# A hybrid attention, convolution and ConvFFN encoder on one core: SyncE's transfers in program order, and a new slot plan for the up product

## The chip, the cores and the metric

The kernel runs on one core of one Trainium2 chip, as one launch. The metric is device time in microseconds (us), lower is better. The same kernel is run several times and the median is taken; one further execution is profiled.

## The reference

Two layers over a residual stream of 1024 tokens by 1024 channels, float32. Cut to the part that the change touches:

```python
for l in range(DEPTH):                       # 2
    h = _rmsnorm(x, g_mix[l])
    p = h @ w_in[l]                          # latents, rope key, a and gate
    ...                                      # 8 heads of latent attention -> y_attn
    u = silu(layernorm(dwconv31(a * sigmoid(gt))))
    x = x + concatenate([y_attn, u]) @ w_o[l]
    h2 = _rmsnorm(x, g_ffn[l])
    z = _dwconv(h2 @ w_up[l], w_dw_ffn[l], b_dw_ffn[l])      # 1024 x 5632, 3 taps
    zg, zv = jnp.split(z, 2, axis=-1)                        # 2816 gates, 2816 values
    x = x + (silu(zg) * zv) @ w_down[l]
return _rmsnorm(x, g_final)
```

## The kernel before

**Stages.** Each layer runs projections, attention, the output product (`wo_steps`), the up product with the ConvFFN filter (`up_steps`) and the down product (`down_steps`). Channels lie on the partitions, tokens along the free dimension, in two halves of 512.

**The up product.** `w_up` is cut into 22 pairs of 128 columns: `f` from 0 to 21, with a gate tile (`e` = 0) and a value tile (`e` = 1) for each. Every pair is computed from seven products instead of eight (Strassen's scheme in Winograd's form over two halves of the contraction, gate and value columns): set `i` from 1 to 7 is a combination of halves of the activations (`self.sets[i]`, made once) times a combination of halves of the weights. One product is 12 matmuls of 512 columns: four blocks of the contraction, and for each high x high, high x low and low x high, because each operand is a pair of 16-bit numbers, a high half and a low half.

**Slots.** `feed` lays all products out as `steps`, one product per step (here called a slot). `put(step, rank, f)` hangs other work behind a slot, and within a slot the rank sorts it. `feed` emits slot by slot, so each engine's order is the order written by these numbers. The sequence of products is `seq`: first `START`, the pairs 0 to 3 ("opening pairs"), sets 1 and 2 of all four and then the other sets; then, for `f` from 4, a block of seven slots in the order of `ORDER = (1, 5, 6, 3, 7, 2, 4)`. With m the slot of set 1 of pair `f`, the table `UP` says where its preparation stands:

- `fetch` (m - 18): SyncE loads the raw gate tile (tag "wr", three buffers) and the raw value tile (tag "b", 31 buffers), 512 KB each; profile name `wu`, line L1106.
- `squares` (m - 15 and the next slot): ScalarE squares and sums each tile (`wsq`, L1128), for the scale of the 16-bit parts; `sum5` follows. TensorE's small product `own_total` (`wt`, L1161) and VectorE's `own_scale` (L1133) come at `total` and one slot later.
- for sets 5, 6, 3, 7, 4 two numbers: the slot of the high half (ScalarE, `part_hi`, `w`, L1182) and of the low half (VectorE, `part_lo`, L1185). Sets 1 and 2 are split together (`first_hi`, `first_lo`).
- `sum5`, `sum6`, `sum3`, `sum7`: GpSimd's accumulating loads that add another weight block into the raw tile (L1112), each between the low half of one set and the high half of the next.

The raw gate tile is last read by the low half of set 7; then its buffer is free for pair `f` + 3.

**After a product.** `evict` (the slot after) takes the bank: on ScalarE for sets 1, 5, 6 and 4 (L1228), on VectorE, adding, for 3, 7 and 2 (L1229). Sets 1, 6, 7 and 4 share one accumulating bank, 5 and 3 another, 2 has its own. Then the three-tap filter: its middle tap on ScalarE (L1618), two taps on VectorE (L1624), first for the gate, then, after a silu (L1260), for the value; `close` multiplies both (L1102) and SyncE stores the result (`act<-v`, L1268). For the opening pairs the filters are put off to the slots of `TAPS_AT`. Beside this, sums of the `w_down` weights for the down product are made on VectorE (`sum_load`, `sum_step`: `sd`, L1273 and L1102; stored as `ws`, L1281).

**The down product** is built alike from eleven slots per set. SyncE fetches its weights into the same three "wr" buffers (`fetch`, L1380) and loads the stored activations back (`load`, `ac<-act`, L1362).

**Who sets the order.** Four engines are in `MANUAL`: their instructions stand in the order in which the program emits them. SyncE is not among them; the order of its transfers is chosen by the scheduler. Each engine works in its order and waits at an instruction until what it needs is there.

Of the kernel before, what the change touches and what calls it, by code (L numbers as in the profile page):

```python
# [31 lines left out]
NF = DFF // 128  # L32
# [44 lines left out]
ROW_AT = {2: (7,)}  # L77
ROW_LATE = {0: (6,)}
E = mybir.EngineType
MANUAL = [E.PE, E.DVE, E.Activation, E.Pool]  # L80
LATE_KINDS = (("pool", "both", "act", "pool", "act"), ("pool", "both", "pool", "pool", "pool"))
LATE_COST = {"act": 1.1, "pool": 3.5, "both": 4.8}
NEAR_TAPS = (12, 14, 16, 14)
# [3 lines left out]
NPAR = P_BF + 2 * NF  # L87
HALVES = (slice(0, 512), slice(512, T))
ORDER = (1, 5, 6, 3, 7, 2, 4)
LEFT = 4  # L90
START = [(i, f) for f in range(LEFT) for i in (1, 2)]
START += [(i, f) for i in (5, 3, 6, 7, 4) for f in range(LEFT)]
MIX_AT = {5: (((19, 1), (20, 0.5)), ((20, 0.4), (21, 0.5))), 3: (((23, 0.6), (24, 0.6)), ((24, 0.5), (25, 0.6))),
          6: (((26, 0.6), (27, 0.6)), ((27, 0.5), (28, 0.6))), 7: (((30, 0.6), (31, 0.6)), ((31, 0.5), (32, 0.6))),
# [3 lines left out]
KEPT = 18  # L98
TAIL_STEPS = 6
FIRST_TOTAL = 7  # L100
TOTAL_AT = 32
TAPS_AT = (36, 39, 42, 46), (44, 48, 52, 57)
UP = {'fetch': -18, 'squares': -15, 'total': -13, 1: (-2, -2), 5: (-10, -9), 6: (-5, -4), 3: (0, 1), 7: (2, 3), 4: (-1, 0)}
SUM_AT = (0, 1, 2, 6)
LEFT_AT = {5: (15, 16, 18, 19), 6: (19, 21, 22, 23), 3: (24, 25, 26, 27), 7: (25, 31, 33, 34), 4: (37, 38, 39, 40)}
ENDS = (slice(512, 768), slice(768, T))
LEAD_HEADS = 3
# [26 lines left out]
class Encoder:  # L134
# [257 lines left out]
    def run(self):  # L392
# [11 lines left out]
        carry = None  # L404
        with self.tc.manual_schedule(engines=set(MANUAL)):
            for l in range(DEPTH):
# [687 lines left out]
    def up_steps(self, l, steps, put):  # L1094
        nc, a = self.nc, self.a
        left, right = HALVES
        seq = START + [(i, f) for f in range(LEFT, NF) for i in ORDER if (i, f) not in START]
        base = len(steps)
        at = {p: base + q for q, p in enumerate(seq)}
        self.kept = {}  # L1100
        raw, wts, zs, st, sums, scale, back, nback = defaultdict(dict), {}, defaultdict(dict), {}, {}, {}, {}, {}
# [28 lines left out]
        def scales(ps, out, w):  # L1130
            ps = ps.rearrange("p (f e) -> p f e", e=2)
            scale, back, nback, v, h = (out[:, i * w:(i + 1) * w] for i in range(5))
            nc.vector.tensor_reduce(out=v, in_=ps, op=ALU.add, axis=AX.X)  # L1133
            self.half_exponent(h, v)
            self.power(scale, h, -1.0, 204.0)
            for o, at in ((back, self.back), (nback, self.nback)):
                nc.vector.tensor_scalar(out=o.bitcast(I32), in0=h.bitcast(I32), scalar1=EXPONENT, scalar2=at, op0=ALU.mult, op1=ALU.add)
            return scale, back, nback

        def first_total():  # L1140
            ps = self.bank(f"wt{l}", (128, 2 * LEFT))
            tags = self.banks[1][0]
            tags.insert(0, tags.pop())
            nc.tensor.matmul(ps, self.ones, st["sums"], start=True, stop=True)
            parts = scales(ps, self.cp.tile([128, 5 * LEFT], F32, name=f"wt{l}", tag="wt", bufs=1), LEFT)
            for f in range(LEFT):
                scale[f], back[f], nback[f] = (t[:, f:f + 1] for t in parts)
# [97 lines left out]
        def filter_start(f, e):  # L1245
            z = zs[f]
            z["ov"[e]] = o = self.blk(f"{'ov'[e]}{l}_{f}")
            z["in", e] = z.pop("gv"[e]) if e == 0 else z["src"]
            self.conv_start(l, e * NF + f, o, z["in", e], 0, T)

        def filter_tap(f, e, t):
            z = zs[f]
            self.conv_tap(l, e * NF + f, z["ov"[e]], z["in", e], 0, T, t)

        def keep(f):
            zs[f]["src"] = zs[f].pop("v")

        def silu(f):
            o = zs[f]["o"]
            nc.scalar.activation(out=o, in_=o, func=AF.Silu)  # L1260

        def close(f):
            z = zs.pop(f)
            sub(z["v"], z["v"], z["o"], ALU.mult)
            if f >= KEPT:
                self.kept[f] = z["v"]
                return
            nc.sync.dma_start(out=self.actd[l][f], in_=z["v"])  # L1268

        def sum_load(j):  # L1270
            sums[j] = [self.blk(f"sd{l}_{j}{e}") for e in range(2)]
            for e, t in enumerate(sums[j]):
                nc.sync.dma_start(out=t, in_=a["w_down"][l, j + e * (NF // 2)])  # L1273

        def sum_step(j, n):
            p, q = sums[j]
            o, x = ((p[:, left], p[:, right]), (p[:, right], q[:, right]), (q[:, right], p[:, left]), (q[:, left], q[:, right]))[n]
            sub(o, o, x, ALU.add)
            if n == 3:
                for e, t in enumerate(sums.pop(j)):  # L1280
                    nc.sync.dma_start(out=self.wsd[l][j, e], in_=t)  # L1281

        def at_step(m, rank, g, *args):
            put(m, rank, lambda: g(*args))
# [11 lines left out]
        for f in range(LEFT):  # L1296
            at_step((13, 13, 15, 15)[f], 6 + f, sum5, f)
            for i, ms in LEFT_AT.items():
                m, g = ms[f], f % 2
# [4 lines left out]
        for q, (i, f) in enumerate(seq):  # L1304
            n = base + q
            steps.append(lambda i=i, f=f: product(i, f))
            m = EVICT.get((i, f), n + 1)
            put(int(m), m % 1 * 10, lambda i=i, f=f: evict(i, f))
        for f in range(LEFT, NF):
            n = m = at[1, f]  # L1310
            for e in range(2):
                at_step(m + UP["fetch"], 5 + e / 10, fetch, f, e, "b" if e else "wr")
                at_step(m + UP["squares"] + e, 2, own_squares, f, e)
            at_step(m + UP["squares"] + 1, 2.1, sum5, f)
            at_step(max(m + UP["total"], TOTAL_AT), 0.4, own_total, f)
            at_step(max(m + UP["total"], TOTAL_AT) + 1, 0.5, own_scale, f)
            for i in (5, 6, 3, 7, 4):
                hi, lo = (max(m + o, TOTAL_AT + 1) for o in UP[i])
                at_step(hi, 3.6, part_hi, i, f)
# [7 lines left out]
        for f in range(NF):  # L1327
            n = max(at[2, f], at[3, f], at[6, f]) + 1
            n = n if f >= LEFT else TAPS_AT[0][f]
            put(n, 3, lambda f=f: filter_start(f, 0))  # L1330
            put(n + 1, 3, lambda f=f: filter_tap(f, 0, 0))
            put(n + 2, 3, lambda f=f: filter_tap(f, 0, 2))
            put(n + 3, 4, lambda f=f: silu(f))
            m = max(at[7, f], at[4, f]) + 2 if f >= LEFT else TAPS_AT[1][f]
            put(m, 2.9, lambda f=f: keep(f))
            put(m, 3, lambda f=f: filter_start(f, 1))
            put(m + 1, 3, lambda f=f: filter_tap(f, 1, 0))
            put(m + 2, 3, lambda f=f: filter_tap(f, 1, 2))
            put(max(m + 3, n + 5), 3, lambda f=f: close(f))
        for j in range(NF // 2):  # L1340
            n = at[1, 7 + j * 13 // 11]
            put(n - 4, 5, lambda j=j: sum_load(j))
            for i, d in enumerate(SUM_AT):
                put(n + d, 4, lambda j=j, i=i: sum_step(j, i))

    def down_steps(self, l, steps, put):
        nc, a = self.nc, self.a
# [63 lines left out]
        def product(i, j, ms=range(4), cs=done):  # L1411
            b, t = pairs[i, j], BANK_SET[i]
            for m in ms:
                if i in (1, 5, 2) and j == 0:
                    ps[t, m] = self.pp.tile([128, 512], F32, name=f"pd{l}_{i}{m}", tag=f"d{4 * t + (m + 2) % 4}", bufs=1)
                for s, (p, q) in enumerate(((0, 0), (0, 1), (1, 0))):
                    nc.tensor.matmul(ps[t, m][:, cs], w[i, j][p][:, m * 128:(m + 1) * 128], b[:, q, cs],  # L1417
                                     start=(i in (1, 5, 2) and j == 0 and s == 0), stop=(j == half - 1 and s == 2),
                                     skip_group_check=i in (6, 7, 4, 3))
# [19 lines left out]

        order = [(i, j) for i in ORDER for j in range(half)]  # L1440
        at = {p: base + q for q, p in enumerate(order)}
# [27 lines left out]
        for c in range(2 if last else 0):  # L1469
            for m in range(4):  # L1470
                steps.append(lambda c=c, m=m: [product(4, j, (m,), cols[c]) for j in range(tail, half)])
        for i in ORDER[:-1]:
            for m in range(4):
# [581 lines left out]
```

## Time and profile before

| | us |
|---|---|
| median of 3 runs | 2264.53 |
| lowest and highest of them | 2263.61, 2265.57 |
| the profiled execution: its own time | 2264.85 |
| its span (first to last instruction) | 2263.0 |
| granted TensorE clock, mean | 0.999 of full speed |

Busy shares of the span: TensorE 99%, its weight loads 67%, VectorE 80%, ScalarE 60%, GpSimd 29%. In the profile a line such as L1221 is a line of the kernel; `out<-in` are tile names without buffer numbers; what stands behind "<-" in an idle time is the engine and the tile that ended it. In rows in order of time the columns are the start, the duration, the engine, the line, the operation, its tiles and shapes, the count of merged instructions, and in brackets the idle time ahead of it. SPq rows are SyncE's issues, and a merged row spans the first to the last of them with the waits between.

### The profile page before, as it was taken

How to read it: one execution, taken by the hardware profiler on the slowest of the kernel's cores; microseconds unless marked ns; L12 is line 12 of the kernel's file. 1: busy time of each engine (PE TensorE's matmuls, PEld its weight loads, DVE VectorE, ACT ScalarE, POOL GpSimd, SP SyncE). 2: the span in 40 equal slices, each digit the busy share in tenths (PEclk: the TensorE clock that was granted, in tenths of full speed). 3: DMA queues.
4: the chain of work that ended last, by engine and by line, in shares of the span. 5: the costliest groups of instructions: out<-in, count | busy, mean ns of one | idle time of the engine just before them, and what ended most of it. 6: DMA issues, size and time to landing. Idle time of an engine off the chain costs nothing.

```text
span 2263.0 us, 30127 instructions
## 1 busy us (share of the span) xinstructions
PE 2233.7 (99%) x10762; PEld 1511.4 (67%) x10762; DVE 1809.0 (80%) x2484; ACT 1349.5 (60%) x2076; POOL 659.2 (29%) x632
## 2 busy tenths in 40 slices
PE   9999999999999999999999999999999999999998
PEld 8887777784444444788888877777744444448887
DVE  7989888878888887776559798887798887878665
ACT  5355987646766665544533568786467666655444
POOL 1222788511111111001412237864111111110032
PEclk9999999999999999999999999999999999999999
DMA  6887998955589796835968989878646888868356
GB/s 192 171 182 251 196 205 176 267 152 117 134 231 257 202 255 163 295 102 138 210 142 167 212 252 208 182 158 246 168 108 158 236 244 223 241 162 284 103 123 171
DMA packets 176967, 434.81 MB, mean 192 GB/s; under 512 B 24769, under 2 KB 32817, under 8 KB 176817
## 3 DMA queue, kind: packets, MB, share of 16 engines
q0 software_dynamic: 79520, 176.31, 41.7%
q1 hardware_dynamic: 97008, 256.04, 33.5%
q8 instruction: 85, 1.39, 0.3%
q14 instruction: 66, 0.53, 0.1%
q10 hardware_dynamic: 288, 0.53, 0.1%
HBM read 293.56 MB, written 80.40 MB: 165 GB/s over the span
## 4 chain that ended last, share of the span: by engine, by line
PE 71%; DVE 12%; DMA 8%; ACT 4%; issue 4%; POOL 1%; SPq 0%; DVEq 0%; POOLq 0%; ACTq 0%
PE pd L1417 18%; PE p L1221 18%; PE s L1677 7%; DMA wu<-in_w_up 5%; PE po L956 5%; PE t L1717 4%; PE o L1740 4%; PE pa L234 2%; DVE w L1185 2%; DVE v L1624 2%; PE pg L234 2%; PE pg L552 2%; DVE conv L1892 2%; PE pq L234 1%; DVE sd L1102 1%
## 5 line engine op out<-in xcount | busy, mean ns | idle before, releaser
L1221 PE MATMUL p<-b,w 128*128 128x512 f16 x3696 | 807.6, 379 | 16.6 <-DVE w L1185 12.1
L1221 PEld LDWEIGHTS <-w 128*128 128x128 f16 x3696 | 360.3, 99 | 449.0 <-DVE w L1185 22.5
L1417 PE MATMUL pd<-ab,wd 128*128 128x512 f32 (+1 forms) x1920 | 422.7, 382 | 0.0
L1417 PEld LDWEIGHTS pd<-ab,wd 128*128 128x128 f32 x1920 | 350.7, 188 | 69.7 <-DVE ab L1612 0.4
L1112 POOL DMA_DIRECT2D wu<-in_w_up x176 | 153.7, 945 | 757.2 <-DVE w L1185 370.4
L1677 PE MATMUL s<-k,q 96*128 96x512 f32 x768 | 208.2, 406 | 3.3 <-DVE qn L748 3.0
L1128 ACT ACTIVATE wsq<-wu 128x1024 f16<-128x1024 f32 x88 | 92.3, 1050 | 179.8 <-DMA wu<-in_w_up 159.3
L1720 DVE SCALAR_TENSOR_TENSOR pt<-t,pt 128x512 f16<-128x512 f32 x256 | 164.7, 684 | 39.2 <-ACT pt L1719 38.6
L1185 DVE SCALAR_TENSOR_TENSOR w<-wu,wf,w 128x512 f16<-128x512 f32 (+1 forms) x216 | 177.4, 834 | 14.6 <-ACT w L1182 14.6
L1909 POOL TENSOR_TENSOR late<-gate,par 128x1014 f32<-128x1014 f32 (+12 forms) x79 | 172.4, 2182 | 12.8 <-PE pn L234 7.1
L1719 ACT ACTIVATE pt<-t 128x512 f16<-128x512 f32 x256 | 139.2, 595 | 56.8 <-PE t L1717 55.9
L1182 ACT ACTIVATE w<-wu,wf 128x512 f16<-128x512 f32 (+1 forms) x216 | 162.5, 783 | 6.9 <-DMA wu<-in_w_up 6.8
L1679 DVE TENSOR_REDUCE mx<-s 128x1 f32<-128x1024 f32 x128 | 155.6, 1215 | 1.3 <-PE s L1677 1.3
L1624 DVE SCALAR_TENSOR_TENSOR o<-zg,par,o 128x1023 f32<-128x1023 f32 x88 | 112.6, 1280 | 53.9 <-ACT o L1618 53.7
L1677 PEld LDWEIGHTS s<-k,q 96*128 96x128 f32 x768 | 135.8, 189 | 26.4 <-DVE qn L748 3.4
L1892 DVE SCALAR_TENSOR_TENSOR conv<-gate,par,conv 128x1009 f32<-128x1009 f32 (+7 forms) x112 | 142.2, 1274 | 3.7 <-ACT conv L614 1.0
L1687 ACT ACTIVATE p<-s,mx 128x1024 f32<-128x1024 f32 x128 | 143.3, 1119 | 2.6 <-DVE mx L1679 2.2
L1610 ACT CAST ab<-ac 128x512 fp32r<-128x512 f32 x130 | 80.0, 616 | 101.6 <-DVE ac L1351 64.3
L1717 PEld LDWEIGHTS t<-ident,p 128*128 128x128 f32 x1024 | 119.7, 141 | 25.1 <-DVE yt L1747 0.8
L1740 PE MATMUL o<-pt,v 128*128 128x512 f16 x512 | 132.8, 381 | 1.3 <-DVE pt L1720 1.1
L1717 PE MATMUL t<-ident,p 128*128 128x128 f32 x1024 | 133.2, 273 | 0.1
L918 POOL DMA_DIRECT2D wd<-in_w_down x44 | 31.8, 724 | 323.6 <-PE pd L1417 322.4
(2114 smaller groups left out, 3834.9 us busy)
## 6 DMA issues: line engine op xcount, KB each, us to landing
wu<-in_w_up SPq DMA_DIRECT2D x98, 512.0 KB, 5.9
wu<-in_w_up POOLq DMA_DIRECT2D x176, 256.0 KB, 4.7
sd<-in_w_down SPq DMA_DIRECT2D x44, 512.0 KB, 6.6
ws<-sd SPq DMA_DIRECT2D x44, 512.0 KB, 4.2
wd<-in_w_down POOLq DMA_DIRECT2D x88, 256.0 KB, 5.5
act<-v SPq DMA_DIRECT2D x36, 512.0 KB, 4.5
ac<-act SPq DMA_DIRECT2D x72, 256.0 KB, 5.8
wo<-in_w_o POOLq DMA_DIRECT2D x64, 256.0 KB, 7.5
```

Source lines behind the costliest of these rows:

```text
L1182: nc.scalar.activation(out=t, in_=src, func=AF.Copy, scale=scale[f])
L1185: nc.vector.scalar_tensor_tensor(out=t, in0=src, scalar=scale[f], in1=hi, op0=ALU.mult, op1=ALU.subtract)
L1221: nc.tensor.matmul(ps, w[p][:, k * 128:(k + 1) * 128], b[:, q], start=(i in (1, 5, 2) and k == 0 and t == 0), stop=(k == 3 and t == 2), sk ...
L1417: nc.tensor.matmul(ps[t, m][:, cs], w[i, j][p][:, m * 128:(m + 1) * 128], b[:, q, cs], start=(i in (1, 5, 2) and j == 0 and s == 0), stop= ...
L1624: self.nc.vector.scalar_tensor_tensor(out=o[:, a:b], in0=z[:, at + a:at + b], scalar=self.par[l][:, tap:tap + 1], in1=o[:, a:b], op0=ALU.m ...
L1677: nc.tensor.matmul(ps[:, cs], q[i][0:96, qs], k[j][0:96, cs], start=(s == 0), stop=(s == 2))
L1679: nc.vector.tensor_reduce(out=mx, in_=ps, op=ALU.max, axis=AX.X, negate=True)
L1717: nc.tensor.transpose(tp[:, i, qi * 128:(qi + 1) * 128], st["p"][2 * qp + qi][:, kt * 128:(kt + 1) * 128], self.ident)
L1720: nc.vector.scalar_tensor_tensor(out=lo, in0=tp, scalar=P_SCALE, in1=hi, op0=ALU.mult, op1=ALU.subtract)
L1740: nc.tensor.matmul(po, v[2 * c + i][:, h // 2, e, :], pt[s][:, 2 * (c % 2) + i, :], start=(c == 0 and i == 0 and s == 0), stop=(c == 3 and ...
L1892: self.nc.vector.scalar_tensor_tensor(out=y[:, lo:hi], in0=u[:, lo + s:hi + s], scalar=self.tap(l, j, t), in1=y[:, lo:hi], op0=ALU.mult, o ...
L1909: self.nc.gpsimd.tensor_tensor(out=p[:, lo:hi], in0=u[:, lo + s:hi + s], in1=self.tap(l, j, t).broadcast_to([128, hi - lo]), op=ALU.mult)
```

## The change

- SyncE is added to `MANUAL`, so its transfers stand in the order in which the program emits them, over the whole program. For that the two stores of `up_steps` get slots of their own: `act_store` and `sum_store`, one slot (`STORE_LAG`) after the work whose result they store.
- Blocks of the up product run in the order 1, 2, 6, 5, 7, 3, 4 (`UP_ORDER`); the down product keeps `ORDER`. The slots of the weights' halves are set anew in `UP`: sets 5, 6, 3 and 4 one slot later, set 7 one slot earlier. The squares and the total come one slot later; the loads stay at m - 18.
- `TAPS_AT`: gate filters of the opening pairs at 35, 37, 40, 46 instead of 36, 39, 42, 46, value filters at 41, 47, 54, 60 instead of 44, 48, 52, 57.
- `START` begins with set 1 of pairs 0 and 1, then set 2 of both, instead of alternating.

```diff
-MANUAL = [E.PE, E.DVE, E.Activation, E.Pool]
+MANUAL = [E.PE, E.DVE, E.Activation, E.Pool, E.SP]
...
 ORDER = (1, 5, 6, 3, 7, 2, 4)
+UP_ORDER = (1, 2, 6, 5, 7, 3, 4)
 LEFT = 4
-START = [(i, f) for f in range(LEFT) for i in (1, 2)]
+START = [(i, f) for i, f in ((1, 0), (1, 1), (2, 0), (2, 1), (1, 2), (2, 2), (1, 3), (2, 3))]
 START += [(i, f) for i in (5, 3, 6, 7, 4) for f in range(LEFT)]
...
-TOTAL_AT = 32
-TAPS_AT = (36, 39, 42, 46), (44, 48, 52, 57)
-UP = {'fetch': -18, 'squares': -15, 'total': -13, 1: (-2, -2), 5: (-10, -9), 6: (-5, -4), 3: (0, 1), 7: (2, 3), 4: (-1, 0)}
+TOTAL_AT = 33
+TAPS_AT = (35, 37, 40, 46), (41, 47, 54, 60)
+UP = {'fetch': -18, 'squares': -14, 'total': -12, 1: (-2, -2), 5: (-9, -8), 6: (-4, -3), 3: (1, 2), 7: (1, 2), 4: (0, 1)}
 SUM_AT = (0, 1, 2, 6)
+STORE_LAG = 1
...
-        seq = START + [(i, f) for f in range(LEFT, NF) for i in ORDER if (i, f) not in START]
+        seq = START + [(i, f) for f in range(LEFT, NF) for i in UP_ORDER if (i, f) not in START]
...
-            nc.sync.dma_start(out=self.actd[l][f], in_=z["v"])
+            st["act", f] = z["v"]
+
+        def act_store(f):
+            if f < KEPT:
+                nc.sync.dma_start(out=self.actd[l][f], in_=st.pop(("act", f)))
...
             sub(o, o, x, ALU.add)
-            if n == 3:
-                for e, t in enumerate(sums.pop(j)):
-                    nc.sync.dma_start(out=self.wsd[l][j, e], in_=t)
+
+        def sum_store(j):
+            for e, t in enumerate(sums.pop(j)):
+                nc.sync.dma_start(out=self.wsd[l][j, e], in_=t)
...
             put(max(m + 3, n + 5), 3, lambda f=f: close(f))
+            put(max(m + 3, n + 5) + STORE_LAG, 3, lambda f=f: act_store(f))
...
                 put(n + d, 4, lambda j=j, i=i: sum_step(j, i))
+            put(n + SUM_AT[-1] + STORE_LAG, 4, lambda j=j: sum_store(j))
```

## The prediction

> **What bounds the kernel now.** I read the page first (busy shares, chain, costliest groups), then TensorE's order of time through the two up products, then the other engines around one stall.
>
> ```profile
> PE 2233.7 (99%) x10762; PEld 1511.4 (67%) x10762; DVE 1809.0 (80%) x2484; ACT 1349.5 (60%) x2076; POOL 659.2 (29%) x632
> ...
> PE pd L1417 18%; PE p L1221 18%; PE s L1677 7%; DMA wu<-in_w_up 5%; PE po L956 5%; PE t L1717 4%; PE o L1740 4%; PE pa L234 2%; DVE w L1185 2%; DVE v L1624 2%; PE pg L234 2%; PE pg L552 2%; DVE conv L1892 2%; PE pq L234 1%; DVE sd L1102 1%
> ```
> ```profile
> L1221 PE MATMUL p<-b,w 128*128 128x512 f16 x3696 | 807.6, 379 | 16.6 <-DVE w L1185 12.1 <-ACT zg L1228 3.0 <-DVE b L1034 1.3
> L1417 PE MATMUL pd<-ab,wd 128*128 128x512 f32 x1776 | 404.4, 390 | 0.0
> ```
>
> TensorE is busy 99% of the span, so its own stream is the bound. All that an edit of the order can win is idle time, and of that the up product (L1221) has 16.6 us, the down product (L1417) none. Yet the chain holds loads of up weights (wu) for 5%: something feeds the up product late. TensorE's order of time through both layers' up products:
>
> ```profile
> 507.09 4.28 PE L1221 MATMUL p<-b,w 128*128 128x512 f16 x19
> 512.02 3.83 PE L1221 MATMUL p<-b,w 128*128 128x512 f16 x17 [0.65 <-DVE b L1034]
> 515.68 0.95 PE L261 MATMUL rf_1p<-ones_r,fss 128*128 128x1 f32 x8
> 516.49 2.75 PE L1221 MATMUL p<-b,w 128*128 128x512 f16 x12
> 519.08 0.60 PE L311 MATMUL rf_1s<-ident,rf_1y 128*128 128x128 f32 x4
> 519.51 33.83 PE L1221 MATMUL p<-b,w 128*128 128x512 f16 x156
> ...
> 587.27 5.77 PE L1221 MATMUL p<-b,w 128*128 128x512 f16 x26
> 594.64 12.69 PE L1221 MATMUL p<-b,w 128*128 128x512 f16 x58 [1.60 <-DVE w L1185]
> ...
> 645.67 18.29 PE L1221 MATMUL p<-b,w 128*128 128x512 f16 x84
> ...
> 663.94 18.29 PE L1221 MATMUL p<-b,w 128*128 128x512 f16 x84
> ...
> 738.50 5.77 PE L1221 MATMUL p<-b,w 128*128 128x512 f16 x26 [0.61 <-ACT zg L1228]
> 745.13 12.69 PE L1221 MATMUL p<-b,w 128*128 128x512 f16 x58 [0.86 <-DVE w L1185]
> ...
> 919.97 5.38 PE L1417 MATMUL pd<-ab,wd 128*128 128x512 f32 x22
> ```
> ```profile
> 1627.70 4.28 PE L1221 MATMUL p<-b,w 128*128 128x512 f16 x19
> ...
> 2040.30 4.91 PE L1417 MATMUL pd<-ab,wd 128*128 128x512 f32 x20
> ```
>
> One slot (a product of 12 matmuls) takes 12 x (33.83 - 0.38)/155 = 2.59 us. An undisturbed block of seven slots takes 663.94 - 645.67 = 18.27 us with its two small sums. A stage without a stall is then 28 opening slots (72.5) + 18 blocks (328.9) + the root's two small steps (0.81 + 0.43) = 402.6 us. The stages took 919.97 - 507.09 = 412.9 and 2040.30 - 1627.70 = 412.6, so the stalls cost 10.3 + 10.0 = **20.3 us**. That is the most this change can win there. The pattern is plain: after a block's small sum come 26 matmuls (products of sets 6, 3 and the first two matmuls of 7), then a wait for DVE's low half of set 7's weights.
>
> One stall followed back (SyncE, ScalarE and VectorE in order of time):
>
> ```profile
> 720.40 1.19 SPq L1273 DMA_DIRECT2D sd<-in_w_down  x2
> 721.69 3.72 SPq L1106 DMA_DIRECT2D wu<-in_w_up  x2
> ```
> ```profile
> 722.87 1.75 ACT L1182 ACTIVATE w<-wu,wf 128x512 f16<-128x512 f32 x2
> 732.76 1.06 ACT L1128 ACTIVATE wsq<-wu 128x1024 f16<-128x1024 f32 x1 [8.13 <-DMA wu<-in_w_up]
> 733.72 0.19 ACT L1128 ACTIVATION_READ_ACCUMULATOR wsq<-wu 128x1 f32 x1
> 733.82 1.22 ACT L1618 ACTIVATE o<-zg,par 128x1024 f32<-128x1024 f32 x1
> ```
> ```profile
> 724.26 0.75 DVE L1185 SCALAR_TENSOR_TENSOR w<-wu,wf,w 128x512 f16<-128x512 f32 x1
> ...
> 735.07 1.28 DVE L1624 SCALAR_TENSOR_TENSOR o<-zg,par,o 128x1023 f32<-128x1023 f32 x1 [3.68 <-ACT o L1618]
> ...
> 744.33 0.74 DVE L1185 SCALAR_TENSOR_TENSOR w<-wu,wf,w 128x512 f16<-128x512 f32 x1
> ```
>
> The low half of set 7 ends at 725.0 and frees the raw buffer; SyncE's second wu load, the gate half, goes out then, behind two sd loads and the value half; it lands 7.7 us later at 732.7. ScalarE has stood 8.13 us before the squares (wsq) of it, with the gate filter's start queued behind. VectorE therefore starts the filter's taps at 735.07, still owes four slots of work, and finishes set 7's low half at 745.07; TensorE resumes at 745.13. Lateness of a load, then, turned into lateness of the last low half, for which there is no spare slot: it is made in slot 3 and used in slot 4.
>
> **The change part by part.** I count slots from the start of a block.
>
> *Loads and squares.* The gate half's load needs the raw buffer, so it moves with set 7's low half, from the end of slot 3 to slot 2. The prices:
>
> ```profile
> L1185 DVE SCALAR_TENSOR_TENSOR w<-wu,wf,w 128x512 f16<-128x512 f32 x57 | 42.5, 745 | 2.8 <-ACT w L1182 2.8
> L1624 DVE SCALAR_TENSOR_TENSOR v<-zv,par,v 128x1023 f32<-128x1023 f32 x24 | 30.6, 1276 | 0.0
> ...
> L1229 DVE SCALAR_TENSOR_TENSOR zg<-p,wf,zg 128x512 f32<-128x512 f32 x23 | 17.2, 749 | 0.9 <-PE p L1221 0.7 <-issue 0.2
> L1102 DVE TENSOR_TENSOR sd<-sd,sd 128x512 f32<-128x512 f32 x22 | 15.0, 683 | 0.0
> L1102 DVE TENSOR_TENSOR v<-v,o 128x1024 f32<-128x1024 f32 x12 | 14.6, 1215 | 0.0
> ```
> ```profile
> wu<-in_w_up SPq DMA_DIRECT2D x98, 512.0 KB, 5.9
> wu<-in_w_up POOLq DMA_DIRECT2D x176, 256.0 KB, 4.7
> sd<-in_w_down SPq DMA_DIRECT2D x44, 512.0 KB, 6.6
> ```
>
> In slot 2 VectorE will do set 2's eviction (0.75), a tap (1.28) and the low halves of 3 and 7 (2 x 0.745): done 3.5 us into slot 2. In the block above slot 2 began at 719.5, so the load could go at 723.0, 2.1 us sooner, and first of its group: the changed order is gate half, two sd, value half. The squares move to slot 0 of the next block behind one eviction, 732.4 + 0.7 = 733.1. The lead is 10.1 us against a landing of 5.9 (median) to 7.7 (that block): covered. The value half goes some 1.6 us later (the two sd issues took 1.19), at 724.6, and is wanted in slot 1, at 735.7: lead 11.1. The trace does not show four such loads in this order. Low end: 5.9, all overlapped. High end: in turn, 7.7 + 2 x 6.6 + 5.9 = 26.8, which would be late by 14. I take 8, near the low end, since the 7.7 row is already the last load of such a group of four. Then ScalarE waits for no load. The Trainium skill (DMA: Bandwidth & Descriptors, section "Anatomy of one DMA — SWDGE (gpsimd) path") fits a transfer as about 2.0 us plus bytes over 436 GB/s, an estimate of 6.8 us for the four, and by that all 20.3 us would be won; but it would also give 3.2 us for one load, where the rows here say 5.9, so the measurement decides.
>
> *Set 7's weights.* High and low half move one slot earlier (1 and 2) and product 7 stays in slot 4: the low half is done at 3.5 us, product 7 begins at 2 x 2.59 = 5.2 us from slot 2. 1.7 us of cover where there was none; this is the edit that takes the 12.1 us group away. Its raw sum (an accumulating POOL load, 4.7 us) has two slots to land instead of three, 5.2 us; POOL's queue now has it ahead of the next block's set-6 sum, so it does not wait for that set's low half, and the reader stands behind an eviction, a square and a filter start (0.7 + 1.06 + 1.22) in ScalarE's slot 1, 8.2 us in all: nothing. If it lands late all the same, ScalarE stands, and the 1.7 us of cover go first.
>
> *Set 2 second, set 5 and 3 later.* Evictions on VectorE move from slots 4, 5, 6 to 2, 5, 6; each bank still has one slot between a product's end and its reuse, as before: nothing by itself. Before, VectorE's slots 0 to 3 held 2.7 to 2.8 us each against 2.59; now slot 2 holds 3.5 + 0.68 (a sum) = 4.2, slots 3 and 4 hold about 2.1 and 2.0. From slot 2: 4.2 + 2.1 + 2.0 = 8.3, then the eviction of 7 (0.75) at 9.1, before product 4 overwrites that bank at 10.4. Cover 1.3 us. ScalarE's slot 1 gets two evictions' and filters' work (about 4.3 us) and its slot 2 only one silu; eviction 6 in slot 3 keeps its slot.
>
> *Put-off taps, opening.* The first blocks lost most (1.60 idle in the first). There VectorE also filters the four opening pairs: two taps and a product each, 2 x 1.28 + 1.22 = 3.8 us. Before, three of these fell in the first two blocks; now one goes ahead of the blocks and the rest one per block. A block without sums has 17.2 - 2.7 = 14.5 us of VectorE (4 taps, 5 low halves, a double one of 1.28, 3 evictions, 4 sums, a product, 0.9 of scales make 17.2); plus 3.8 is 18.3 on 18.27. Full, so I leave 1 us of stalls per layer here, and 0.5 elsewhere. The opening's second product becomes (1,1), so set 2's late low half (the 0.65 idle; 512.02 - 507.09 - 19 x 0.216 = 0.83) has a slot of cover: all won, counted above.
>
> *SyncE in program order, everywhere else.* Every transfer stays, only the order changes. In attention the next head's loads move behind the small rb load, half a head before their use: nothing. The y loads go ahead of the first wu loads, whose squares come two slots later: nothing. In the down product half the act loads move behind the weight fetches:
>
> ```profile
> SPq L1380 <- DVE wd L1612: 85.6, 26, 12.0
> ```
> ```profile
> ac<-act SPq DMA_DIRECT2D x72, 256.0 KB, 5.8
> ```
>
> An act load is placed five slots (13.6 us at 2.72 us) ahead of its combination, that three slots ahead of the product. A fetch in front may wait 12.0 (the longest): 12.0 + 5.8 = 17.8 against 13.6 + 8.2 = 21.8. Nothing, with 4 us to spare.
>
> **Sum.** 20.3 - 3.0 = 17.3 us, off the profiled execution's 2264.85 (span 2263.0): 2247.5. It lies 0.3 above the median of the runs, 2264.53; I predict **2247.3** for the median. Ends: 20.3 won gives 2244.2.
>
> **The rivals.**
> 1. *Half.* The value half lands late (the high end's direction) or set 7's raw sum does: ScalarE still stands, though with a slot more of cover. For it: that many bytes close together. Against: 11.1 us of lead. Half of 20.3: 2254.4.
> 2. *The stalls only move.* VectorE is the cause by its sheer load, and the low half is merely late elsewhere. For: 17.2 of 18.27 us. Against: undisturbed blocks run at 18.27 now. 2264.5.
> 3. *Slower: slot 2's burst.* Eviction 7 comes after product 4 should begin. It decides once VectorE enters slot 2 over 1.3 us late, in all 36 blocks, and each further us costs 36. A lag of 2.3: -17.3 + 36 = +18.7, 2283. For: the burst of 4.2 us is new. Against: 1.1 us of slack per block brings it back.
> 4. *Slower: SyncE held up in the down product.* A waiting fetch holds all loads behind it, and this stage has nothing to win. It decides over 4 us beyond the longest wait. A second 12.0 us wait in front makes the load 8 us late, in products 5 and 6 of both layers: -17.3 + 4 x 8 = +14.7, 2279. The Trainium skill (same page and section) says that waits are served on the issuing sequencer, not by the DMA engines. The SyncE rows of the down product agree (26 waits, 85.6 us).
>
> That the order doesn't change is excluded: in the changed program's order gate half, sd, sd, value half stand as said.
>
> **How the numbers follow.** A measurement can tell about 0.2%, 4.5 us. Forecast 0.62, half 0.17, moved 0.09, burst 0.07, held up 0.05. Faster: forecast and half, 0.79. Same 0.09. Slower 0.12. The range takes forecast and half with their bounds: from the whole 20.3 and 1 us of runs, 2243, to half less 6 us, 2260.
>
> **What would show it.** Right: the up stages at 403 to 405 us; TensorE's idle before L1221 under 4 us; ScalarE's 8.13 us waits before wsq gone; the gate half's load first of its group; the down product's idle still 0.0. Wrong: idle before L1221 named by an eviction (zv) or by set 7's low half again; ScalarE standing before w on a wu load; idle in L1417.

## The result, and the profile after

| kernel | median, us | lowest to highest | up product, layer 0 | layer 1 | span |
|---|---|---|---|---|---|
| before | 2264.54 | 2263.61 to 2265.57 | 412.88 | 412.60 | 2263.0 |
| after | 2245.83 | 2244.61 to 2246.53 | 402.39 | 402.39 | 2243.5 |

The change makes the kernel faster by 18.7 us: a ratio of 0.9917, 95% interval 0.990 to 0.9934. The forecast was 2247.3 (2243 to 2260), 17.3 us of gain. An up product's length is read in TensorE's order of time, from its first matmul to the down product's first.

The chain by engine from the page of the kernel before, then busy shares and the same from the page of the kernel after (line numbers have moved: L1221 is now L1223, L1417 is L1426, L1185 is L1187, L1128 is L1130):

```profile
PE 71%; DVE 12%; DMA 8%; ACT 4%; issue 4%; POOL 1%; SPq 0%; DVEq 0%; POOLq 0%; ACTq 0%
```
```profile
PE 2229.5 (99%) x10762; PEld 1512.3 (67%) x10762; DVE 1808.6 (81%) x2484; ACT 1359.0 (61%) x2076; POOL 657.9 (29%) x632
...
PE 92%; DVE 4%; DMA 3%; ACT 1%; issue 0%; POOL 0%; SPq 0%; DVEq 0%; POOLq 0%; ACTq 0%
```

The busy shares hardly move; loads of up weights are gone from the chain, of which TensorE now is 92% instead of 71%. The group of the up product, kernel after:

```profile
L1223 PE MATMUL p<-b,w 128*128 128x512 f16 x3696 | 803.6, 379 | 0.0
```

Its idle time went from 16.6 us to 0.0. TensorE's order of time, kernel after:

```profile
508.11 7.94 PE L1223 MATMUL p<-b,w 128*128 128x512 f16 x36
...
590.07 18.29 PE L1223 MATMUL p<-b,w 128*128 128x512 f16 x84
...
608.34 18.29 PE L1223 MATMUL p<-b,w 128*128 128x512 f16 x84
...
699.67 18.29 PE L1223 MATMUL p<-b,w 128*128 128x512 f16 x84
...
717.94 18.29 PE L1223 MATMUL p<-b,w 128*128 128x512 f16 x84
...
910.50 19.67 PE L1426 MATMUL pd<-ab,wd 128*128 128x512 f32 x85
...
1618.45 7.94 PE L1223 MATMUL p<-b,w 128*128 128x512 f16 x36
...
2020.84 19.44 PE L1426 MATMUL pd<-ab,wd 128*128 128x512 f32 x84
```

Every block takes 18.27 us, no row has an idle time, and 910.50 - 508.11 = 2020.84 - 1618.45 = 402.39. The two stages give 10.49 + 10.21 = 20.70 us. The span fell by 19.5 only: the first up product starts 1.02 us later than before (more on that below), and the stretch between the two takes 707.95 instead of 707.73.

The block that the prediction followed, after the change (SyncE, VectorE and ScalarE in order of time):

```profile
718.76 0.33 SPq L1108 DMA_DIRECT2D wu<-in_w_up  x1
719.14 0.90 SPq L1279 DMA_DIRECT2D sd<-in_w_down  x2
720.08 0.43 SPq L1108 DMA_DIRECT2D wu<-in_w_up  x1
```
```profile
717.32 1.41 DVE L1187 SCALAR_TENSOR_TENSOR w<-wu,wf,w 128x512 f16<-128x512 f32 x2
...
723.38 0.75 DVE L1231 SCALAR_TENSOR_TENSOR zv<-p,wf,zv 128x512 f32<-128x512 f32 x1 [0.38 <-PE p L1223]
```
```profile
726.69 1.24 ACT L1627 ACTIVATE o<-zg,par 128x1024 f32<-128x1024 f32 x1 [3.63 <-DVE zg L1231]
...
729.08 1.05 ACT L1130 ACTIVATE wsq<-wu 128x1024 f16<-128x1024 f32 x1
...
731.67 1.05 ACT L1130 ACTIVATE wsq<-wu 128x1024 f16<-128x1024 f32 x1
```

The low halves of sets 3 and 7 are done at 718.7, the gate half goes out first, at 718.76, and the squares begin 10.3 us later without a wait. Over the program, ScalarE's waits before the squares (total, times, longest), before and after:

```profile
ACT wsq L1128 <- DMA wu<-in_w_up: 159.3, 31, 8.1
```
```profile
ACT wsq L1130 <- DMA wu<-in_w_up: 10.0, 3, 4.7
```

VectorE reaches the eviction of set 7 before TensorE is done with the product: it waits 0.38 us for TensorE, not the other way round.

### The profile page after: what moved, and what is told of

Read it like the earlier page. It is cut to its first block, busy times and chain, and to the rows that moved or that the text cites. A ratio compares the mean times of both kernels' runs of the same rounds, so it can differ in the third digit from the quotient of the medians.

```text
span 2243.5 us, 30143 instructions
## 1 busy us (share of the span) xinstructions
PE 2229.5 (99%) x10762; PEld 1512.3 (67%) x10762; DVE 1808.6 (81%) x2484; ACT 1359.0 (61%) x2076; POOL 657.9 (29%) x632
## 4 chain that ended last, share of the span: by engine, by line
PE 92%; DVE 4%; DMA 3%; ACT 1%; issue 0%; POOL 0%; SPq 0%; DVEq 0%; POOLq 0%; ACTq 0%
PE p L1223 36%; PE pd L1426 19%; PE s L1686 8%; PE po L958 7%; PE t L1726 5%; PE o L1749 4%; PE pa L236 2%; PE pg L236 2%; DVE conv L1901 2%; PE pg L554 2%; PE pq L236 1%; PE pkv L236 1%; PE pa L554 1%; DMA wo<-in_w_o 1%; PE pv L1662 1%; PE pn L236 1%
## 5 line engine op out<-in xcount | busy, mean ns | idle before, releaser
L1223 PE MATMUL p<-b,w 128*128 128x512 f16 x3696 | 803.6, 379 | 0.0
L1223 PEld LDWEIGHTS <-w 128*128 128x128 f16 x3696 | 361.6, 99 | 427.0 <-DVE w L1187 0.6
L1426 PE MATMUL pd<-ab,wd 128*128 128x512 f32 (+1 forms) x1920 | 422.7, 382 | 0.0
L1426 PEld LDWEIGHTS pd<-ab,wd 128*128 128x128 f32 x1920 | 350.7, 188 | 69.7 <-DVE ab L1621 0.4
L1187 DVE SCALAR_TENSOR_TENSOR w<-wu,wf,w 128x512 f16<-128x512 f32 (+1 forms) x216 | 176.9, 833 | 4.0 <-ACT w L1184 4.0
L1627 ACT ACTIVATE o<-zg,par 128x1024 f32<-128x1024 f32 x44 | 54.5, 1239 | 135.1 <-DVE zg L1231 135.1
```

The costliest lines, as they stand in the source:

```text
L1187: nc.vector.scalar_tensor_tensor(out=t, in0=src, scalar=scale[f], in1=hi, op0=ALU.mult, op1=ALU.subtract)
L1223: nc.tensor.matmul(ps, w[p][:, k * 128:(k + 1) * 128], b[:, q], start=(i in (1, 5, 2) and k == 0 and t == 0), stop=(k == 3 and t == 2), sk ...
```

## The experiments

Which part of the change brings this? The forecast named the late gate half; the rivals below are set 7's place in the block, and SyncE's order by itself. Medians alone can't part kernels that lie 1 to 3 us from each other. The lengths of the up products can: in the four kernels in which TensorE never waits there, they come out at 402.39 in both layers, while the rest of the program moves by more than 1 us between traces (the first up product begins at 505.9 to 509.0). Each length is from the one trace of its kernel. Each ratio is to the kernel before as it was timed together with that run (medians 2263.39 to 2264.18).

| kernel | median, us | ratio to before, 95% interval | up product, layer 0 | layer 1 |
|---|---|---|---|---|
| `sp_only` | 2299.43 | 1.016 [1.0146, 1.0174] | 429.54 | 428.42 |
| `plan_only` | 2243.29 | 0.9913 [0.9899, 0.9926] | 402.39 | 402.39 |
| `set7_only` | 2252.74 | 0.9955 [0.9942, 0.9967] | 407.09 | 409.02 |
| `set7_squares` | 2252.17 | 0.9944 [0.9932, 0.9957] | 405.81 | 406.14 |
| `set7_back` | 2257.26 | 0.9972 [0.9961, 0.9982] | 407.81 | 408.11 |
| `plan_set7_back` | 2254.23 | 0.9953 [0.994, 0.9965] | 407.16 | 407.16 |
| `squares_back` | 2244.89 | 0.9915 [0.9901, 0.9929] | 402.39 | 402.39 |
| `order_back` | 2248.92 | 0.9936 [0.9924, 0.9949] | 404.08 | 403.72 |
| `taps_back` | 2247.33 | 0.9926 [0.9913, 0.994] | 403.34 | 403.34 |
| `start_back` | 2246.17 | 0.9924 [0.9911, 0.9936] | 403.20 | 403.21 |
| `low3_thrice` | 2249.80 | 0.9939 [0.9926, 0.9951] | 404.69 | 404.68 |
| `y_later` | 2244.10 | 0.9912 [0.9896, 0.9927] | 402.39 | 402.39 |

**SyncE's order alone, on the old slots.**

```diff
-MANUAL = [E.PE, E.DVE, E.Activation, E.Pool]
+MANUAL = [E.PE, E.DVE, E.Activation, E.Pool, E.SP]
+STORE_LAG = 1      # act_store, sum_store as in the change; all slots as before
```

> The kernel before with SyncE's transfers in the program's order and the stores put off by a slot; the slot plan stays. Late load (the forecast's theory): the gate half still waits for set 7's low half at the end of slot 3 and lands 5.5 to 7.7 us after it, and the squares still want it about 8 us earlier, so ScalarE's waits before wsq stay at 6 us or more and most of the 20.3 us of stalls stays: 2258 to 2268 us. Order alone (rival: it is the place of the gate half in SyncE's queue that counts): the waits go, about 2247 us. No spare slot (rival: set 7's low half is made one slot ahead of its use, whatever the loads do): 2264 us. In all three the 1.0 us wait for yt at the end of the first attention, seen after the change, should be here if the early y loads make it.

Measured: slower by 36 us, which none of the three had. VectorE, SyncE and ScalarE in order of time, ScalarE's waits, and the group of the up product:

```profile
694.01 0.74 DVE L1187 SCALAR_TENSOR_TENSOR w<-wu,wf,w 128x512 f16<-128x512 f32 x1
```
```profile
694.83 0.33 SPq L1108 DMA_DIRECT2D wu<-in_w_up  x1
...
696.22 0.47 SPq L1108 DMA_DIRECT2D wu<-in_w_up  x1
```
```profile
699.98 1.06 ACT L1130 ACTIVATE wsq<-wu 128x1024 f16<-128x1024 f32 x1 [4.70 <-DMA wu<-in_w_up]
...
705.18 1.06 ACT L1130 ACTIVATE wsq<-wu 128x1024 f16<-128x1024 f32 x1 [1.73 <-DMA wu<-in_w_up]
```
```profile
ACT wsq L1130 <- DMA wu<-in_w_up: 189.1, 55, 6.8
```
```profile
L1223 PE MATMUL p<-b,w 128*128 128x512 f16 x3696 | 815.3, 380 | 39.8 <-ACT zg L1230 20.7 <-DVE w L1187 17.5 <-DVE b L1036 1.3
```

The gate half is now first of its group and waits for its buffer until 694.8, the end of set 7's low half; the two sd and the value half, which in the kernel before went ahead of it, stand behind it. So ScalarE waits twice in a block instead of once (55 waits instead of 31), and TensorE's idle time goes from 16.6 to 39.8 us. Set 7's place is the same as before, and the loads come later: that speaks against the theory by which the loads do not matter, and for the late load, whose range for this run, 2258 to 2268 us, is missed all the same. A transfer that is not ready holds up the queue behind it. The Trainium skill (DMA: Bandwidth & Descriptors, section "Anatomy of one DMA — SWDGE (gpsimd) path") says that waits are served on the issuing sequencer; this trace agrees, the value half goes out 1.4 us after the gate half and not before it.

**The slots alone, SyncE's order left to the scheduler.**

```diff
-MANUAL = [E.PE, E.DVE, E.Activation, E.Pool, E.SP]
+MANUAL = [E.PE, E.DVE, E.Activation, E.Pool]
```

> The kernel after, but SyncE's transfers are ordered by the scheduler again, so the gate half is the last load of its group, behind two sd and the value half. Late load: the slots carry the gain, since the buffer comes free about 2.1 us sooner and the squares come 2.6 us later, a lead of about 8.5 us against a landing of 5.5 to 7.7: ScalarE's waits before wsq stay under 2 us, TensorE's idle in the up products under 3 us, 2244 to 2249 us. Order alone: most of the stalls come back, 2258 us or more. No spare slot: as after, 2245 us. The 1.0 us wait for yt should be gone if the early y loads make it.

Measured: the whole gain, with the gate half last of its group. SyncE's order brings nothing to the up product once the slots are moved.

**Set 7 alone.**

```diff
-... 3: (0, 1), 7: (2, 3), 4: (-1, 0)}
+... 3: (0, 1), 7: (1, 2), 4: (-1, 0)}
```

> The kernel before with set 7's weights made one slot earlier and nothing else. No spare slot: the 1.7 us of cover and the earlier free buffer are all it takes, stalls of 0 to 3 us, 2245 to 2249 us. Late load: the gate half lands about 2.3 us sooner but the squares are not later, so ScalarE still stands 4 to 6 us before them and the taps are still late, against a cover of 1.7 us: 4 to 12 us of stalls stay, 2249 to 2257 us. Order alone: unchanged unless the scheduler's order moves the gate half, about 2264 us.

Measured: the stages give 5.79 + 3.58 = 9.4 us. ScalarE's waits, the group of the up product, TensorE's longest wait of layer 0, and ScalarE just before it:

```profile
ACT wsq L1128 <- DMA wu<-in_w_up: 85.9, 30, 4.4
```
```profile
L1221 PE MATMUL p<-b,w 128*128 128x512 f16 x3696 | 806.3, 379 | 8.7 <-ACT zv L1228 7.4 <-DVE b L1034 1.3
```
```profile
758.18 15.70 PE L1221 MATMUL p<-b,w 128*128 128x512 f16 x72 [2.26 <-ACT zv L1228]
```
```profile
756.84 0.72 ACT L1182 ACTIVATE w<-wu,wf 128x512 f16<-128x512 f32 x1 [4.38 <-DMA wu<-in_w_up]
757.47 0.67 ACT L1228 ACTIVATE zv<-p,wf 128x512 f32<-128x512 f32 x1
```

ScalarE still stands before the squares, in 30 places, as the late-load theory said; but TensorE no longer waits for set 7's low half anywhere. It waits for an eviction by ScalarE, and the longest such wait of each layer (2.26 and 2.35 us) stands behind another late load: ScalarE had stood 4.38 and 4.47 us before the high half of a weight, waiting for up weights. That is one of the signs by which the prediction said that it would be wrong.

**Set 7 back**, from the kernel after, with SyncE in program order and without:

```diff
-... 7: (1, 2), 4: (0, 1)}
+... 7: (2, 3), 4: (0, 1)}      # plan_set7_back: and MANUAL without E.SP
```

> The kernel after with set 7's weights back in slots 2 and 3. Late load: the gate half's load goes out 2.3 us later, a lead of about 7.8 us against a landing of 5.5: ScalarE's waits stay under 1 us, VectorE is on time in slot 3, stalls of 0 to 4 us, 2245 to 2250 us. No spare slot: the 12.1 us of idle put down to that low half comes back, 2255 to 2260 us. Order alone: as after, 2246 us.

> Set 7's weights back in slots 2 and 3, with SyncE's order left to the scheduler, so that the gate half goes last and holds up no other load of its group. No spare slot: TensorE waits for set 7's low half again, as with SyncE in the program's order, 2253 to 2258 us. SyncE's queue (rival: with set 7 put back it was the blocked gate half that made the value half land after 10.3 us and ScalarE late): the value half goes out ahead of it, ScalarE stands for the gate half at most, and most of the 11 us is not lost, 2244 to 2249 us.

Measured: 5.4 and 5.7 us per layer are lost again, 4.8 and 4.8 with the scheduler's order. The late-load theory allowed 4 us in all for `set7_back`, so in the changed plan lateness of loads is not the whole story. `plan_set7_back` shows it at its plainest (TensorE, VectorE, and ScalarE's waits):

```profile
686.45 15.28 PE L1223 MATMUL p<-b,w 128*128 128x512 f16 x70 [0.17 <-DVE w L1187]
...
701.71 3.18 PE L1223 MATMUL p<-b,w 128*128 128x512 f16 x14
705.06 15.28 PE L1223 MATMUL p<-b,w 128*128 128x512 f16 x70 [0.17 <-DVE w L1187]
```
```profile
699.25 0.75 DVE L1231 SCALAR_TENSOR_TENSOR zg<-p,wf,zg 128x512 f32<-128x512 f32 x1 [1.43 <-PE p L1223]
...
704.25 1.41 DVE L1187 SCALAR_TENSOR_TENSOR w<-wu,wf,w 128x512 f16<-128x512 f32 x2
```
```profile
ACT wsq L1130 <- DMA wu<-in_w_up: 9.7, 4, 2.9
```

ScalarE's waits before the squares are gone (4 in the program, against 31 before), and still TensorE waits for set 7's low half in 12 blocks of each layer: in the first one about 1.0 us are lost, in the other eleven 0.34 each, as here, where the block takes 705.06 - 686.45 = 18.61 us instead of 18.27. In slot 2 VectorE first evicts set 2 and waits for that product's end, until 699.25; from there on it is never idle. Slot 3 starts at 701.71, and VectorE ends the low half (the first of the two in the row) at 705.0, 3.3 us later; product 7 starts 2.59 us after 701.71 and wants the low half at its third matmul, 3.0 us after. It is late by arithmetic, and no load holds VectorE up here. This is a property of the changed order, though: in the kernel before, VectorE evicts nothing in slots 2 and 3, and with set 7 in the same two slots the blocks without a stall take 18.27 us. SyncE's order adds the rest; in `set7_back` a value half took 10.3 us (SyncE, then ScalarE):

```profile
688.62 0.43 SPq L1108 DMA_DIRECT2D wu<-in_w_up  x1
```
```profile
698.95 1.06 ACT L1130 ACTIVATE wsq<-wu 128x1024 f16<-128x1024 f32 x1 [0.79 <-DMA wu<-in_w_up]
```

**The squares**, added to set 7 alone, and taken out of the kernel after:

```diff
-'squares': -15, 'total': -13      # set7_squares: before, with set 7 at (1, 2)
+'squares': -14, 'total': -12      # and TOTAL_AT = 33
```
```diff
-'squares': -14, 'total': -12      # squares_back: from after
+'squares': -15, 'total': -13
```

> The kernel before with two edits alone: set 7's weights one slot earlier and the squares one slot later; SyncE's order, the order of the sets, taps and opening as before. If these two carry the gain in the blocks, what is left is the opening's own (0.65 us at its second product and about 1.6 us in the first blocks, per layer): 2245 to 2249 us. If the order of the sets or the taps are needed as well, stalls of 4 us or more stay in the blocks, 2249 to 2253 us; 2253 us, as with set 7 alone, if the squares bring nothing.

> The kernel after with the squares (and the total) one slot earlier, as before. Late load: the value half has a lead of 11.1 less 2.6, 8.5 us, against the 10.3 us that it took at the worst with set 7 put back; ScalarE stands up to 2 us before wsq in each block, against 1.7 us of cover for set 7's low half: 0 to 8 us of stalls, 2246 to 2254 us. No spare slot (set 7's place alone decides): as after, 2246 us, whatever ScalarE waits. If it is slower, the waits before wsq must be back among ScalarE's.

Measured: with set 7 early, later squares take ScalarE's waits before wsq from 85.9 to 10.9 us, and of the up products 1.3 and 2.9 us. Put back to the old slot in the finished kernel, they cost nothing. ScalarE's waits of `squares_back`:

```profile
ACT wsq L1130 <- DMA wu<-in_w_up: 18.0, 15, 3.1
```

Eleven of these waits lie in the up products, none longer than 2.2 us, and TensorE is idle there for 0.0. So the finished plan has room for short waits; waits of 4 to 8 us, as in the kernel before, did not come back here and are not tested by this run.

**Order, taps and opening**, each put back alone in the kernel after:

```diff
-UP_ORDER = (1, 2, 6, 5, 7, 3, 4)
+UP_ORDER = ORDER                                              # order_back
-TAPS_AT = (35, 37, 40, 46), (41, 47, 54, 60)
+TAPS_AT = (36, 39, 42, 46), (44, 48, 52, 57)                  # taps_back
-START = [... (1, 0), (1, 1), (2, 0), (2, 1), ...]
+START = [(i, f) for f in range(LEFT) for i in (1, 2)]         # start_back
```

> The kernel after with the old order of the sets in a block (1, 5, 6, 3, 7, 2, 4); weights, squares, taps and opening stay where the change put them. The forecast's step: the order is worth nothing by itself, both up products keep 402.4 us, 2245.8 us. Rival: set 2's bank and its eviction (set 7 and squares alone had left 3.4 and 3.7 us per layer, with waits for ScalarE's eviction zv in the first blocks) need the new order: 1 to 3 us per layer, 2248 to 2252 us.

> The kernel after with the put-off taps of the four opening pairs at their old slots. The forecast's step: VectorE is full in the first blocks (18.3 of 18.27 us), so the old places cost 1 to 2 us per layer there, in the first three blocks alone: 2247.8 to 2249.8 us. Rival (set 7's cover of 1.7 us takes it up): nothing, 2245.8 us.

> The kernel after with the opening's products in pairs (1,0) (2,0) (1,1) (2,1) as before. The forecast's step: the second product waits again for set 2's late low half, 0.83 us per layer and nowhere else, up products of 403.2 us each: 2247.5 us. Rival (the wait is hidden or moves to the next product): 2245.8 us.

Measured in the up products: the order 1.69 and 1.33 us, the taps 0.95 and 0.95, the opening 0.81 and 0.82. The group of the up product in the three, in this order:

```profile
L1223 PE MATMUL p<-b,w 128*128 128x512 f16 x3696 | 804.2, 379 | 1.7 <-ACT zv L1230 1.2 <-DVE zv L1231 0.5
```
```profile
L1223 PE MATMUL p<-b,w 128*128 128x512 f16 x3696 | 804.0, 379 | 1.6 <-DVE zv L1231 1.6
```
```profile
L1223 PE MATMUL p<-b,w 128*128 128x512 f16 x3696 | 804.0, 379 | 1.3 <-DVE b L1036 1.3
```

The first two wait for evictions (zv), all of them in the first blocks, where the opening's filters are made up; the third is the opening's own wait. Together the three are worth 3.0 + 1.9 + 1.6 = 6.5 us. `set7_squares` is 3.42 + 3.75 = 7.2 us longer than the kernel after; besides these three it lacks SyncE's order, which `plan_only` shows to be worth nothing in the kernel after, and the later slots of sets 5, 6, 3 and 4, which no run moves alone. If the parts simply add, 0.7 us are left for those slots.

**More work on VectorE in slot 2.**

```diff
+                for _ in range(2 * (i == 3)):
+                    at_step(lo, 3.5, part_lo, i, f)
```

> The kernel after with set 3's low half computed three times over in each block, ahead of set 7's low half in slot 2: 1.33 us more of VectorE per block, in the slot that the burst rival names. The forecast's step: set 7's low half ends 1.33 us later against 1.7 of cover and the next eviction of set 7 at 10.4 us against product 4 at 10.4, so no single block stalls by it; but a block with sums holds 18.5 us of VectorE against 18.27, and 11 such blocks per layer pile up 2.9 us, of which 1 to 3 us per layer come out: 2247 to 2252 us. Burst rival: each of 36 blocks stalls by 0.3 to 1 us, 2256 to 2282 us. VectorE has room (neither): 2245.8 us.

Measured: 2.30 and 2.29 us, inside the forecast's 1 to 3 per layer, but not by its reasons. VectorE's busy time in one block with sums, kernel after and then `low3_thrice` (the stretch and its length, VectorE's busy time with its instructions, the granted clock, the share of the DMA engines, GB/s):

```profile
699.95:718.22 18.27, 15.77 (x24) 1.00 0.91 260
```
```profile
699.95:718.22 18.27, 17.11 (x26) 1.00 0.89 262
```

A block with sums holds 15.8 us of VectorE, with the extra work 17.1: it fits, and these blocks stay at 18.27. The loss falls in the first blocks, those with the opening's filters:

```profile
634.30 10.52 PE L1223 MATMUL p<-b,w 128*128 128x512 f16 x48 [1.73 <-DVE zv L1231]
```

**The y loads behind the first wu loads.** In the kernel after there is one new wait, ahead of the first up product (TensorE, then ScalarE):

```profile
422.42 0.50 PE L1945 MATMUL lnp<-lns0h,ones_r 128*128 128x512 f32 x1 [1.03 <-DVE yt L1756]
```
```profile
420.24 0.63 ACT L199 ACTIVATE wo<-wo 128x512 fp32r<-128x512 f32 x1 [1.70 <-DMA wo<-in_w_o]
```

```diff
-        put(-3, 0, load_x)
+        put(0, 6, load_x)
```

> The kernel after with the 12 other y loads placed behind the first three wu loads again, as SyncE had them before. If the early y loads make the wo load late that ScalarE stands before at the end of the first attention (1.70 us, TensorE 1.03 us), that idle goes and the time falls by 1.0 us against the kernel after, to 2244.8 us; if not, it stays at 2245.8 us. The trace tells it, the time alone can't.

Measured: the wait is absent. But of the eight traces with early y loads it stands in three only (the kernel after, `sp_only` with 0.97 and `squares_back` with 0.21 us); none of the six with late y loads has it. So the wait goes with the early loads here but not always, and its 1 us is below what the times here can tell. This stays open.

No kernel beats the one after by more than that: `plan_only` and `y_later` have the same up products, and their intervals overlap with its own.

## Why the prediction was right, and where it was not

- **The bound and what could be won: right.** A stage without stalls was put at 402.6 us and is 402.39; the stalls at 20.3 and were 20.7. That the sum of 17.3 came close to the measured 18.7 is in part luck: 3.4 us more than that were won in the up products, and 1.2 us, put at nothing, were lost outside them.
- **What would stay: too large.** The 3.0 us left in the sum for the first blocks and elsewhere came to 0.0. The term that was mis-sized is VectorE's block: 17.2 us was summed from the rows' durations, but neighbours overlap. The two low halves at 717.32, of 0.745 each, take 1.41 together; the window of a whole block says 15.8. So the first blocks were not full with one opening filter each; the busiest stretch of a block's length there, in the kernel after:

```profile
626.61:644.88 18.27, 17.55 (x25) 1.00 0.82 226
```

The prediction had 18.3 for it. At the old places those filters do cost 0.95 per layer.
- **The step about the late load: right for the later blocks, not for the first two.** The prediction read the chain from the gate half's landing through ScalarE to set 7's low half in one block. The trace of the kernel before lets one test it on all of them. VectorE's waits for the start of the gate filter, which ScalarE makes behind the squares (total, times, longest), two of them, and TensorE after the first of the two:

```profile
DVE o L1624 <- ACT o L1618: 53.7, 30, 3.7
```
```profile
829.59 1.28 DVE L1624 SCALAR_TENSOR_TENSOR o<-zg,par,o 128x1023 f32<-128x1023 f32 x1 [2.94 <-ACT o L1618]
...
866.60 1.28 DVE L1624 SCALAR_TENSOR_TENSOR o<-zg,par,o 128x1023 f32<-128x1023 f32 x1 [2.01 <-ACT o L1618]
```
```profile
839.65 12.69 PE L1221 MATMUL p<-b,w 128*128 128x512 f16 x58 [0.86 <-DVE w L1185]
```

Nine of the 30 waits are 2.26 us or longer, and behind each of these TensorE waits for set 7's low half; in eight of them it waits for 2.06 to 2.11 us less than VectorE did (here 2.94 - 0.86 = 2.08). The 21 waits up to 2.02 us pass without a stall, except in two blocks where ScalarE stood 2.8 and 3.0 us before a high half, for up weights again. The stalls of these eleven blocks are 9.2 of the 16.6 us. The first two blocks of each layer lose 1.60 and 1.40 us, 6.0 in all, with no wait of ScalarE for a load over 0.9 us ahead of them in the stage; the prediction put these down to the opening's filters, and no run tests that in the old plan. The remaining 1.3 us are the opening's own wait. `sp_only`, with later loads and set 7 in its old place, agrees: its stalls grow from 20.7 to 53.2 us.
- **The remedy for it: set 7's slot, not the queue.** The earlier slot of set 7 frees the buffer sooner and gives its low half cover; the runs do not part these two. `plan_set7_back` shows only that the changed order needs the cover even where no load is late. The kernel before with nothing but later squares was not run, so it is open how much moving the squares alone would have won.
- **Set 7's weights: right.** Forecast 1.7 us of cover and the 12.1 us group gone. In the block above the low half ends at 718.7, slot 3 starts at 717.94 and product 7 one slot later, at 720.5: 1.8 us. Put back, 9.5 to 11.1 us return.
- **Gate half first: the lead was right (10.1 forecast, 10.3 measured), its worth was not.** With the scheduler's order, gate half last, the stage is as long. The fit that the prediction sets beside its own figure, from the Trainium skill (DMA: Bandwidth & Descriptors, section "Anatomy of one DMA — SWDGE (gpsimd) path"), is given there for transfers that GpSimd issues, while these loads are SyncE's. One of them took 5.9 us before and 5.5 after (medians).
- **"By itself nothing" for the order of the sets: wrong**, 3.0 us in both layers, in evictions of the first blocks.
- **The opening: right**, 0.83 forecast, 0.81 and 0.82 measured.
- **SyncE elsewhere: nearly right.** The down product's idle is 0.0. Against "nothing" stands the wait of 1.03 us at the end of the first attention.
- **The rivals.** "Half" did not come: before the squares ScalarE does not wait in either up product, and before the high halves 0.2 us in all. The burst of slot 2 did not come either: set 7's next eviction waits for TensorE, and 1.34 us more of work there moved no steady block. VectorE's sheer load was no bound, with 2.5 us free per block. SyncE held up did happen, not in the down product but in `sp_only`, where the gate half holds the queue: that rival's mechanism was real, and the slots of the same change keep it from being seen.

## What to carry to other kernels

One stall followed back is a guess at the cause: go through all blocks and see whether the stall's length follows the wait's, and from which wait on. Where an operand is made in the slot just before its use, try one slot earlier before reordering loads: here that took away more than any other single edit that was tried. Then add up its engine's work in the new order against the slot's length; and put a queue into program order only where each transfer is ready when it gets to the front. Sum an engine's load from a window over a whole period, not from the durations of its rows.

## What the runs showed of the hardware

The longer rows of VectorE overlap with the next by about 0.08 us (two low halves of 0.745 each take 1.41 together), and the sum over a block's rows (17.2) lies 9% above its busy time (15.8). And the median landing of the stores moved with SyncE's order, kernel before and kernel after:

```profile
ws<-sd SPq DMA_DIRECT2D x44, 512.0 KB, 4.2
```
```profile
ws<-sd SPq DMA_DIRECT2D x44, 512.0 KB, 7.9
```

In the five kernels without SyncE in program order the trace says 3.0 to 4.3 us for them; with it, 7.0 to 11.7. They are issued close behind the block's loads there, in stretches in which the DMA engines are busy for 0.9 of the time; that this is the reason was not tested, and TensorE's idle in the up product is 0.0 all the same.
